# Last chunk of both output projections of a fp32 transformer block: a plain product by token block, each block with its own norm

## The chip, the cores and the metric

The kernel runs on one core of a Trainium2 chip. The metric is the device time of one execution in microseconds. In names of engines: PE is TensorE, DVE is VectorE, ACT is ScalarE, POOL is GpSimd, SP is SyncE, which issues the DMAs.

## What is computed

A block on 1024 latent tokens and 256 context tokens of width 1024, all in fp32. Both feed-forward networks (FFN1 and FFN2) are half-step SwiGLU networks with a hidden width of 2816; between them stands a mixer. FFN2 and the final norm are wanted for the latent tokens only.

```python
def rmsnorm(x, g):
    xf = x.astype(jnp.float32)
    n = xf * lax.rsqrt(jnp.mean(xf * xf, axis=-1, keepdims=True) + EPS)
    return (n * g.astype(jnp.float32)).astype(x.dtype)
...
def swiglu(y, w_in, w_out):
    gate, up = jnp.split(y @ w_in, 2, axis=-1)
    return (jax.nn.silu(gate) * up) @ w_out
```

Per layer: x += gate * swiglu(y) with y the modulated RMSNorm of x (FFN1); then the mixer on a new norm of x; then FFN2 in the same form; then a last RMSNorm to the output. A norm needs the sum of squares over all 1024 features of a token, so it can begin only when the output projection has finished every feature of that token.

## The kernel before

Activations lie transposed: features on partitions, tokens along the free dimension. The latent tokens are two blocks of 512 (tb 0 and 1), the context one of 256 (tb 2). An fp32 product is three products of split operands (high by high, high by low, low by high), each a step of a 128x128 weight piece by 512 columns.

Both projections of an FFN use a scheme of Strassen and Winograd: 7 products of half-size blocks in place of 8. `winograd` (L467) runs the jobs and issues the steps (L479). Its left operands are sums of weight quarters: `unit` (L369) makes them of two loaded pieces, with copies on ScalarE (L389, L393, L396, L403) and sums and differences on GpSimd (L383, L384) for the output projection. Its right operands are sums of the hidden blocks: `combos` (L410) forms them with VectorE and `hl` (L429, L430) splits them; seven tiles of 512 KB per pair are spilled to `hd` (L581).

The output projection runs in chunks of 1, 2, 2, 2, 2, 2 pairs. Each chunk has four jobs, loads its hidden tiles `hc` (L702: 14 of them for two pairs) and, in FFN1, the context's `cc` (L708). Class `Out` says what becomes of the products: VectorE adds each to an accumulator from PSUM (L512, the names a, b, c, f are PSUM banks), the product that several outputs need is summed in `u` and folded into three accumulators in the chunk before the last. In the last chunk it is added three times directly; each output is then finished (L625: x = acc * gate + x), squared on ScalarE and summed over features (`tail`, L461 and L463). Two context products of the last chunk are put off to the end.

After all jobs comes one norm for both blocks: column sums on TensorE (`rstd_cols`, L265, 16 products one column wide), a reciprocal root by 12 small VectorE operations on 8 columns (L279 to L255), its spreading over the partitions on TensorE (L288, 16 products), and then for FFN1 the norm itself (L327 to L334), whose result y the mixer's products `z` take (L356), or for FFN2 the outputs (L1403 to L1414).

The order of instructions on each engine, SyncE's DMA issues included, is decided by a scheduler that simulates a timeline; the pools (32 large tiles d, 7 h, 8 m, 6 PSUM banks for products) limit it. A queue is worked off strictly in its order, so an instruction that waits holds all behind it on that engine.

## Time and profile before

| | us |
|---|---|
| median of 3 runs | 2185.55 (2184.21 to 2193.85) |
| profiled execution | 2185.07 |
| its span in the trace | 2183.3 |
| TensorE busy | 2016.1 (92%) |
| VectorE busy | 1541.3 (71%) |
| ScalarE busy | 832.8 (38%) |
| GpSimd busy | 420.2 (19%) |

The share of busy time is an average over stages with different limits. FFN1's output projection lies from about 645 to 940 us, its last chunk from 868 to 927.5; the mixer follows to about 1475 us and FFN2's first product starts at 1479.0; its output projection lies from about 1919 to 2160, the last chunk from 2110 to 2153.2. The execution's 2185.07 us are the span of 2183.3 and 1.8 us outside the trace.

### The profile page before, as it was taken

How to read it: one execution, taken by the hardware profiler on the slowest of the kernel's cores; microseconds unless marked ns; L12 is line 12 of the kernel's file. 1: busy time of each engine (PE TensorE's matmuls, PEld its weight loads, DVE VectorE, ACT ScalarE, POOL GpSimd, SP SyncE). 2: the span in 40 equal slices, each digit the busy share in tenths (PEclk: the TensorE clock that was granted, in tenths of full speed). 3: DMA queues.
4: the chain of work that ended last, by engine and by line, in shares of the span. 5: the costliest groups of instructions: out<-in, count | busy, mean ns of one | idle time of the engine just before them, and what ended most of it. 6: DMA issues, size and time to landing. Idle time of an engine off the chain costs nothing.

```text
span 2183.3 us, 28555 instructions
## 1 busy us (share of the span) xinstructions
PE 2016.1 (92%) x10820; PEld 1669.9 (76%) x10820; DVE 1541.3 (71%) x2543; ACT 832.8 (38%) x1322; POOL 420.2 (19%) x245
## 2 busy tenths in 40 slices
PE   6799999999999999879999998596999999989995
PEld 2678888888887888757788876474888888867884
DVE  3976665656675779979888376679677786755587
ACT  3633333333342121256556345226344443441222
POOL 0000000000025666422210010200000000065762
PEclk9799999999999999979999899798999999999997
DMA  7033333333369687411111125551444343568852
GB/s 282 24 111 131 116 135 126 121 116 116 116 252 390 251 299 279 156 63 54 40 60 53 35 88 214 205 164 39 164 157 161 118 180 127 194 258 340 307 198 77
DMA packets 115881, 344.86 MB, mean 158 GB/s; under 512 B 12960, under 2 KB 15904, under 8 KB 115744
## 3 DMA queue, kind: packets, MB, share of 16 engines
q1 hardware_dynamic: 115744, 343.04, 42.7%
q8 instruction: 85, 1.39, 0.3%
q14 instruction: 52, 0.43, 0.1%
HBM read 237.60 MB, written 105.38 MB: 157 GB/s over the span
## 4 chain that ended last, share of the span: by engine, by line
PE 67%; DVE 17%; DMA 6%; issue 6%; ACT 3%; POOL 1%; SPq 0%; POOLq 0%; DVEq 0%; ACTq 0%
PE c L479 15%; PE a L479 14%; PE f L479 14%; PE b L479 7%; DVE acc L741 4%; DVE acc L512 2%; DMA ar<-in_wb 2%; PE gc L526 2%; PE gc L525 2%; PE gc L524 2%; DMA hc<-hd 2%; PE row L205 1%; DVE junk L168 1%; DVE hl L430 1%; DVE x L625 1%
## 5 line engine op out<-in xcount | busy, mean ns | idle before, releaser
L384 POOL TENSOR_TENSOR gl<-raw,gh 128x1024 fp32r<-128x1024 f32 x22 | 54.1, 2460 | 1168.8 <-ACT gh L389 1157.2
L168 DVE SCALAR_TENSOR_TENSOR junk<-ar,cr 128x512 bf16<-128x512 f32 x160 | 112.6, 704 | 63.7 <-DMA ar<-in_wb 45.1
L389 ACT ACTIVATE gh<-raw 128x1024 fp32r<-128x1024 f32 x66 | 70.0, 1060 | 197.7 <-PE c L479 70.7
L393 ACT ACTIVATE sh<-s 128x1024 fp32r<-128x1024 f32 x66 | 69.8, 1057 | 167.9 <-PE a L479 94.8
L429 ACT ACTIVATE hl<-g 128x512 fp32r<-128x512 f32 x110 | 67.5, 625 | 159.5 <-DVE g L512 152.0
L479 PE MATMUL f<-hl,uh 128*128 128x512 f32 x528 | 126.8, 389 | 0.0
L479 PE MATMUL c<-hl,sh 128*128 128x512 f32 x352 | 112.5, 397 | 11.8 <-ACT hl L429 9.2
L479 PE MATMUL a<-hl,gh 128*128 128x512 f32 x352 | 114.1, 402 | 8.1 <-ACT hl L429 5.6
L479 PEld LDWEIGHTS f<-hl,uh 128*128 128x128 f32 x528 | 99.1, 188 | 20.6
L479 PE MATMUL b<-hl,gh 128*128 128x512 f32 x352 | 112.0, 395 | 1.0 <-ACT hl L429 1.0
L479 PE MATMUL a<-hl,sh 128*128 128x512 f32 x352 | 110.6, 395 | 1.0 <-ACT g L552 1.0
L479 PE MATMUL f<-hl,th 128*128 128x512 f32 x352 | 110.2, 390 | 1.3 <-ACT hl L429 1.3
L479 PE MATMUL c<-hl,th 128*128 128x512 f32 x352 | 109.0, 391 | 0.1
L741 DVE SCALAR_TENSOR_TENSOR acc<-z,par,acc 128x945 f32<-128x945 f32 (+2 forms) x64 | 95.5, 1512 | 12.3 <-ACT acc L763 11.3
L430 DVE TENSOR_TENSOR hl<-g,hl 128x512 fp32r<-128x512 f32 x110 | 76.7, 712 | 32.5 <-ACT hl L429 32.5
L512 DVE TENSOR_TENSOR u<-c,u 128x512 f32<-128x512 f32 x44 | 30.3, 688 | 96.3 <-ACT u L562 96.3
L142 POOL TENSOR_TENSOR wl<-raw,wh 128x1024 fp32r<-128x1024 f32 x20 | 51.2, 2567 | 241.5 <-ACT wh L141 241.3
L479 PEld LDWEIGHTS c<-hl,sh 128*128 128x128 f32 x352 | 67.1, 191 | 27.5 <-ACT hl L429 9.8
L384 DVE TENSOR_TENSOR sl<-s,sh 128x1024 fp32r<-128x1024 f32 x44 | 53.8, 1224 | 45.7 <-PE gc L525 21.9
L479 PEld LDWEIGHTS a<-hl,gh 128*128 128x128 f32 x352 | 67.0, 194 | 22.3 <-ACT hl L429 6.1
L356 PE MATMUL wo<-ah,wo 128*128 128x512 f32 x128 | 52.1, 408 | 30.0 <-DVE x L1322 28.1
L479 PEld LDWEIGHTS a<-hl,sh 128*128 128x128 f32 x352 | 67.2, 191 | 16.0 <-ACT g L552 1.3
(330 smaller groups left out, 6073.2 us busy)
## 6 DMA issues: line engine op xcount, KB each, us to landing
hd<-hl SPq DMA_DIRECT2D x154, 512.0 KB, 3.6
hc<-hd SPq DMA_DIRECT2D x154, 512.0 KB, 7.7
ar<-in_wb SPq DMA_DIRECT2D x112, 256.0 KB, 3.1
raw<-in_ff1i SPq DMA_DIRECT2D x44, 512.0 KB, 3.9
raw<-in_ff2i SPq DMA_DIRECT2D x44, 512.0 KB, 4.4
raw<-in_ff1o SPq DMA_DIRECT2D x22, 512.0 KB, 5.8
raw<-in_ff2o SPq DMA_DIRECT2D x22, 512.0 KB, 5.1
raw<-in_wa SPq DMA_DIRECT2D x16, 512.0 KB, 10.0
```

The lines of the kernel that those rows point to most:

```text
L142: eng.tensor_tensor(out=lo[:, :n], in0=src[:, :n], in1=hi[:, :n].bitcast(F32), op=ALU.subtract)
L168: i = nc.vector.scalar_tensor_tensor(out=self.junk, in0=w, scalar=1.0, in1=cbc[j], op0=ALU.mult, op1=ALU.mult, accum_out=acc[:, h, dt, j:j ...
L356: m = nc.tensor.matmul(out, a_, xh[k], start=(i == 0), stop=False)
L384: sub = lambda o, x, y: eng.tensor_tensor(out=o, in0=x, in1=y, op=ALU.subtract)
L389: nc.scalar.activation(gh, g, AF.Copy)
L393: nc.scalar.activation(sh, s, AF.Copy)
L429: nc.scalar.activation(t[:, :512], src, AF.Copy)
L430: nc.vector.tensor_tensor(out=t[:, 512:], in0=src, in1=t[:, :512].bitcast(F32), op=ALU.subtract)
L479: mm = lambda x, y, start, stop: nc.tensor.matmul(ps, x, y, start=start, stop=stop, skip_group_check=more)
L512: tt = lambda eng, o, x, y, op: eng.tensor_tensor(out=o, in0=x, in1=y, op=op)
L524: nc.tensor.matmul(ps, hi[:, c], mh, start=i == 0, stop=False)
L741: self.nc.vector.scalar_tensor_tensor(out=o, in0=zv[:, r0 + dr:r1 + dr, c0 + dc:c1 + dc], scalar=self.par[:, tap:tap + 1], in1=o, op0=ALU. ...
```

## The change

The last chunk of both output projections no longer uses the seven products. `last` computes it as a plain product of eight blocks: for each token block it loads four hidden tiles, and for each of eight feature tiles it sums 12 steps of 512 columns in one PSUM bank. `more` adds the result, times the gate, directly from PSUM to x. `halves` replaces `unit` there: the weight pieces are only split, not summed (2 copies, 2 subtracts per unit). As soon as a token block has its eight tiles, `done(tb)` runs its norm alone; the context follows as a third block in FFN1. The folding of `u` and the finishing of the accumulators move from the last chunk to the one before it and to the loop over block 0. The hidden tiles of the last two pairs are spilled as four plain blocks (no `combos`). Accumulators and x tiles are kept by pairs of features and token block.

```diff
+    def halves(self, src, eng, new):
+        nc = self.nc
+        r = {}
+        for x, (i, j) in zip(src, ((1, 2), (0, 4))):
+            x = self.load(x)
+            hi, lo = new("vh", F32R), new("vl", F32R)
+            with self.tc.high_priority():
+                nc.scalar.activation(hi, x, AF.Copy)
+                eng.tensor_tensor(out=lo, in0=x, in1=hi.bitcast(F32), op=ALU.subtract)
+            r[i], r[j] = (hi[:, :512], lo[:, :512]), (hi[:, 512:], lo[:, 512:])
+        return r
...
+        pairs0 = NF // 2 - CHUNKS[-1]
...
+                    if pair >= pairs0:
+                        out(5, b12)
+                        out(7, b22)
+                        return
...
             def p2(s, b):
-                i = add(s.acc(s.m, 0), b, False)
+                i = add(xsum(s.m, 0), b, False)
                 if after_out:
                     after_out(s.j, i)
-                if s.last:
-                    s.finish(s.m, 0)
+                if s.fold:
+                    finish(s.m, 0)
                 if yc:
-                    if s.put_off:
-                        later.append(s.ctx)
-                    else:
-                        s.ctx()
+                    s.ctx()
...
-                if s.last:
-                    for dt, tb in ((m + 4, 1), (m, 1), (m + 4, 0)):
-                        add(s.acc(dt, tb), a, False)
-                else:
-                    add(us[m], a, s.one)
-                add(s.acc(m + 4, 1), c, s.one)
-                add(s.acc(m + 4, 1), f, False)
-                if s.last:
-                    s.finish(m + 4, 1)
+                add(us[m], a, s.one)
+                add(xsum(m + 4, 1), c, s.one)
+                add(xsum(m + 4, 1), f, False)
...
-                add(s.acc(m, 1), c, s.one)
-                add(s.acc(m + 4, 0), f, s.one)
-                if s.chunk == len(CHUNKS) - 2:
-                    for dt, tb in ((m, 1), (m + 4, 0), (m + 4, 1)):
-                        o = s.acc(dt, tb)
-                        tt(nc.vector, o, o, us[m], ALU.add)
-                if s.last:
-                    s.finish(m, 1)
-                    s.finish(m + 4, 0)
-                    tail(m)
-                    tail(m + 4)
+                add(xsum(m, 1), c, s.one)
+                add(xsum(m + 4, 0), f, s.one)
+                if s.fold:
+                    fold_u(m + 4, 0)
+                    finish(m + 4, 0)
...
+        def fold_u(dt, tb):
+            o = xsum(dt, tb)
+            tt(nc.vector, o, o, us[dt % 4], ALU.add)
+        def more(x, ps, dt, j):
+            nc.vector.scalar_tensor_tensor(out=x, in0=ps, scalar=gates()[:, dt, j:j + 1], in1=x,
+                                           op0=ALU.mult, op1=ALU.add)
+        def finish(dt, tb):
+            if (dt // 2, tb) not in xt:
+                xt[dt // 2, tb] = load_x(dt // 2, tb)
+            self.x[dt][tb] = xt[dt // 2, tb][:, dt % 2 * 512:dt % 2 * 512 + 512]
+            more(self.x[dt][tb], xsum(dt, tb), dt, 0)
...
+        def last():
+            kd = CHUNKS[-1]
+            ws = [self.halves(w2[NFO - kd + q], nc.gpsimd, (self.w, self.m)[q % 2 == 0]) for q in range(kd)]
+            tiles = [(q * (4 // kd) + m, i, ws[q], m * kd * P) for q in range(kd) for m in range(4 // kd)
+                     for i in range(2)]
+            rows = lambda w, i, col: [(*w[r], slice(col + k * P, col + k * P + P)) for r in ((1, 2), (0, 4))[i]
+                                      for k in range(kd)]
+            for tb in range(2):
+                right = []
+                for i in ((1, 2), (5, 7))[tb]:
+                    for pair in range(pairs0, NF // 2):
+                        t = self.d("hc", F32R)
+                        nc.sync.dma_start(t.bitcast(F32), hd[pair, names.index(i)])
+                        right.append((t[:, :512], t[:, 512:]))
+                for m, i, w, col in tiles:
+                    dt = m + 4 * i
+                    ps = self.po("o") if i else self.pg("o")
+                    plain(ps, rows(w, i, col), right)
+                    more(self.x[dt][tb], ps, dt, 0)
+                    tail(dt, tb)
+                    if tb == 0:
+                        fold_u(dt, 1)
+                        finish(dt, 1)
+                    elif yc:
+                        finish_c(dt)
+                done(tb)
+            if yc:
+                cs = []
+                for pair in range(pairs0, NF // 2):
+                    t = self.m("cc", F32R)
+                    nc.sync.dma_start(t.bitcast(F32), hc[pair])
+                    cs.append(t)
+                right = [(t[:, h:h + 256], t[:, h + 256:h + 512]) for h in (0, 512) for t in cs]
+                for m, i, w, col in tiles:
+                    dt = m + 4 * i
+                    if i == 0:
+                        pc = self.po("oc")
+                    ps = pc[:, i * 256:i * 256 + 256]
+                    plain(ps, rows(w, i, col), right)
+                    more(self.x[dt][2], ps, dt, 1)
+                done(2)
         p0, n, nj = 0, 0, 0
-        for ci, kd in enumerate(CHUNKS):
+        for ci, kd in enumerate(CHUNKS[:-1]):
...
         self.winograd(jobs)
-        for ctx in later:
-            ctx()
+        last()
...
+        def done1(tb):
+            if "c2" not in late:
+                late["c2"] = self.norm_coef(3, C_N2, 2, "2")
+            self.alloc_y(y2, tb)
+            r = self.rstd(part(2)) if tb == 2 else self.rstd_cols([accs[tb]], 512, 1.0 / 1024.0)
+            self.norm(part(tb), late["c2"], y2, r, pool=True)
...
+        def done2b(tb):
+            bc = self.spread(self.rstd_cols([accs[tb]], 512, 1.0 / 1024.0), 4)
+            b0 = self.h("bc")
+            nc.scalar.activation(b0, bc, AF.Copy)
+            for k in range(NK):
+                g = self.par[:, C_FG + k:C_FG + k + 1]
+                o = self.h("out")
+                if tb and k % 3 == 2:
+                    nc.scalar.activation(o, self.x[k][tb], AF.Identity, scale=g)
+                    nc.gpsimd.tensor_tensor(out=o, in0=o, in1=b0, op=ALU.mult)
+                else:
+                    nc.vector.scalar_tensor_tensor(out=o, in0=self.x[k][tb], scalar=g, in1=bc,
+                                                   op0=ALU.mult, op1=ALU.mult)
+                nc.sync.dma_start(a["out"][k, :, tb * 512:tb * 512 + 512], o)
```

The scheduler places all of this anew. On TensorE at the end of FFN1, before, `st` (column sums), `bc` (spreading) of both blocks stand behind the last context product `oc`, and the mixer's `z` behind them:

```order
L524 MATMUL oc_1157_7588<-cc_1089_7116,uh_1132_7363 128x256
L525 MATMUL oc_1157_7588<-cc_1089_7116,uh_1132_7363 128x256
L526 MATMUL oc_1157_7588<-cc_1089_7116,uh_1132_7363 128x256
L265 MATMUL st_1158_7620<-ones_72,acc_1113_7310 128x1 x4
L265 MATMUL st_1158_7620<-ones_72,acc_1114_7312 128x1 x4
L288 MATMUL bc_1168_7650<-ident_70,r_1159_7629 128x128 x4
L288 MATMUL bc_1185_7699<-ident_70,r_1159_7629 128x128 x4
L356 MATMUL z_1247_7892<-y_1160_7642,wh_1224_7854 128x512
L356 MATMUL z_1248_7919<-y_1160_7642,wh_1229_7862 128x512
```

On TensorE at the same place after, `o` are PSUM banks of the plain product; the first five rows end block 0, `hc_1121` is the first hidden tile of block 1:

```order
L539 MATMUL o_1100_7247<-hc_1081_7105,vh_1076_7095 128x512
L540 MATMUL o_1100_7247<-hc_1081_7105,vh_1076_7095 128x512
L541 MATMUL o_1100_7247<-hc_1081_7105,vl_1077_7096 128x512
L266 MATMUL st_1110_7276<-ones_72,acc_1083_7121 128x1 x4
L289 MATMUL bc_1112_7294<-ident_70,r_1111_7281 128x128 x4
L539 MATMUL o_1125_7343<-hc_1121_7335,vh_1067_7077 128x512
L540 MATMUL o_1125_7343<-hc_1121_7335,vh_1067_7077 128x512
L541 MATMUL o_1125_7343<-hc_1121_7335,vl_1068_7078 128x512
L539 MATMUL o_1129_7364<-hc_1121_7335,vh_1070_7083 128x512
```

The norm of block 0 has moved ahead of all products of block 1.

On SyncE at the end of FFN1, before, the loads of the last hidden tiles and of the last unit's weight halves (`raw` from `in_ff1o`) stood among loads of x and one spill of x to `xd`:

```order
L702 DMA hc_1086_7110<-hd_116_504 128x1024
L702 DMA hc_1087_7112<-hd_116_504 128x1024
L131 DMA raw_1122_7351<-in_ff1o 128x1024
L1355 DMA x_1102_7160<-in_xT 128x512 x2
L126 DMA c_1104_7192<-in_cT 128x1024
L126 DMA c_1105_7193<-in_cT 128x1024
L1355 DMA x_1108_7241<-in_xT 128x512 x2
L1260 DMA xd_7619<-x_1102_7160 128x512
L1355 DMA x_1111_7261<-in_xT 128x512 x2
L1355 DMA x_1119_7345<-in_xT 128x512 x2
L131 DMA raw_1123_7353<-in_ff1o 128x1024
L1355 DMA x_1134_7393<-in_xT 128x512 x2
```

After, the loads of block 1's hidden tiles stand behind eight spills of x tiles of block 0, of which six are shown:

```order
L1311 DMA xd_7751<-x_1032_6707 128x512
L1311 DMA xd_7751<-x_1039_6835 128x512
L1310 DMA xd_7751<-x_1056_6905 128x512
L1310 DMA xd_7751<-x_1063_7033 128x512
L1311 DMA xd_7751<-x_1056_6905 128x512
L1311 DMA xd_7751<-x_1063_7033 128x512
L714 DMA hc_1121_7335<-hd_116_504 128x1024
L714 DMA hc_1122_7337<-hd_116_504 128x1024
L714 DMA hc_1123_7339<-hd_116_504 128x1024
L714 DMA hc_1124_7341<-hd_116_504 128x1024
```

The spills wait for block 0's results, the last one for its last update, and the loads have moved behind them; the weight halves are all issued further ahead.

On TensorE at the end of FFN2, before, the norm of both blocks stands behind the last product:

```order
L479 MATMUL c_2705_17299<-hc_2649_16984,th_2687_17164 128x512 x2
L479 MATMUL c_2705_17299<-hc_2649_16984,tl_2688_17165 128x512
L479 MATMUL f_2706_17300<-hc_2650_16986,uh_2689_17166 128x512 x3
L479 MATMUL f_2706_17300<-hc_2651_16988,uh_2689_17166 128x512 x3
L265 MATMUL st_2712_17355<-ones_72,acc_2670_17114 128x1 x4
L265 MATMUL st_2712_17355<-ones_72,acc_2671_17116 128x1 x4
L288 MATMUL bc_2714_17377<-ident_70,r_2713_17364 128x128 x4
L288 MATMUL bc_2715_17382<-ident_70,r_2713_17364 128x128 x4
```

After, block 0's column sums stand inside the third tile of block 1:

```order
L540 MATMUL o_2660_17162<-hc_2653_17123,vh_2605_16883 128x512
L541 MATMUL o_2660_17162<-hc_2653_17123,vl_2606_16884 128x512
L266 MATMUL st_2640_17072<-ones_72,acc_2621_16927 128x1 x4
L539 MATMUL o_2660_17162<-hc_2654_17125,vh_2605_16883 128x512
L540 MATMUL o_2660_17162<-hc_2654_17125,vh_2605_16883 128x512
```

Its spreading stands 38 rows further on, inside the sixth tile, and only block 1's own norm is left at the end:

```order
L539 MATMUL o_2670_17247<-hc_2655_17127,vh_2614_16901 128x512
L540 MATMUL o_2670_17247<-hc_2655_17127,vh_2614_16901 128x512
L541 MATMUL o_2670_17247<-hc_2655_17127,vl_2615_16902 128x512
L266 MATMUL st_2672_17264<-ones_72,acc_2657_17143 128x1 x4
L289 MATMUL bc_2674_17282<-ident_70,r_2673_17269 128x128 x4
```

Half of the norm has moved from behind the last product to between products.

## Rows read from the trace of the kernel before

**Rows 1.** By stretch: us, busy us per engine, TensorE's clock, DMA share:
```profile
core 0: us, PE busy (x) PEld busy (x) DVE busy (x) ACT busy (x) POOL busy (x), PEclk, DMA share, GB/s
820.00:868.00 48.00, 48.00 (x259) 41.59 (x258) 44.22 (x92) 8.04 (x9) 29.51 (x18) 1.00 0.74 268
868.00:927.50 59.50, 53.27 (x267) 44.40 (x265) 57.34 (x77) 13.04 (x18) 26.51 (x15) 0.94 0.50 175
927.50:960.00 32.50, 16.01 (x58) 13.62 (x58) 27.66 (x52) 17.47 (x28) 9.12 (x6) 0.63 0.29 98
1000.00:1180.00 180.00, 166.10 (x1426) 147.28 (x1425) 160.15 (x204) 96.29 (x182) 30.24 (x12) 0.98 0.16 51
2071.00:2110.00 39.00, 39.00 (x173) 32.02 (x172) 29.63 (x39) 7.42 (x8) 29.32 (x17) 1.00 0.66 251
2110.00:2153.20 43.20, 38.86 (x164) 29.78 (x162) 43.13 (x60) 9.39 (x14) 17.30 (x8) 1.00 0.14 54
2153.20:2183.30 30.10, 7.30 (x32) 6.97 (x32) 16.40 (x34) 8.12 (x13) 7.51 (x6) 0.61 0.36 139
```

**Rows 2.** Chain of waits, steady stretch: start, us, what:
```profile
129.03 2.72 PE c L479 x12
```

**Rows 3.** TensorE's waits, 820 to 962 us: total, times, longest:
```profile
PE st L265 <- DVE acc L463: 11.1, 1, 11.1
PE f L479 <- ACT th L396: 5.8, 1, 5.8
...
PE bc L288 <- DVE r L255: 2.5, 1, 2.5
```

**Rows 4.** Timeline of TensorE, end of FFN1: start, us, instruction, idle before:
```profile
899.71 1.22 PE L479 MATMUL f<-hc,th 128*128 128x512 f32 x2 [5.77 <-ACT th L396]
...
903.70 0.39 PE L479 MATMUL c<-hc,tl 128*128 128x512 f32 x1
...
938.61 3.58 PE L265 MATMUL st<-ones,acc 128*128 128x1 f32 x16 [11.10 <-DVE acc L463]
944.66 3.65 PE L288 MATMUL bc<-ident,r 128*128 128x128 f32 x16 [2.48 <-DVE r L255]
...
958.33 0.39 PE L356 MATMUL ogu<-y,wh 128*128 128x512 f32 x1
```

**Rows 5.** VectorE on acc, 2105 to 2165 us: ns min/median/max, first and last start:
```profile
L512 DVE TENSOR_TENSOR acc<-a,acc x16: 675/680/690, 2109.4 to 2147.4; 128x512 f32<-128x512 f32 x16
L625 DVE SCALAR_TENSOR_TENSOR x<-acc,hg,x x16: 735/744/1691, 2112.2 to 2156.7; 128x512 f32<-128x512 f32 x16
...
L512 DVE TENSOR_TENSOR acc<-acc,u x5: 693/1073/2889, 2105.4 to 2117.3; 128x512 f32<-128x512 f32 x5
```

**Rows 6.** DMA issues of the page: KB each, median us to landing:
```profile
hc<-hd SPq DMA_DIRECT2D x154, 512.0 KB, 7.7
```

**Rows 7.** TensorE's waits, 2040 to 2160 us:
```profile
PE c L479 <- DVE acc L512: 2.6, 3, 2.0
PE f L479 <- DVE acc L512: 1.3, 1, 1.3
```

**Rows 8.** Timeline of VectorE, the last outputs:
```profile
2177.28 2.24 DVE L1412 SCALAR_TENSOR_TENSOR out<-x,par,bc 128x512 f32<-128x512 f32 x3 [0.55 <-DMA out_x<-out]
```

**Rows 9.** TensorE's waits, 630 to 680 us (FFN1, start of the output projection):
```profile
PE oc L524 <- DVE u L512: 2.2, 1, 2.2
PE a L479 <- DMA hc<-hd: 1.9, 1, 1.9
PE f L479 <- DVE acc L512: 0.9, 1, 0.9
```

**Rows 10.** TensorE's waits, 1915 to 1965 us (FFN2, start of the output projection):
```profile
PE c L479 <- ACT acc L607: 3.9, 1, 3.9
PE f L479 <- DVE u L512: 1.1, 1, 1.1
```

**Rows 11.** Timeline of ScalarE, end of FFN2:
```profile
2156.81 0.63 ACT L461 ACTIVATE sq<-x 128x512 f32<-128x512 f32 x1 [0.74 <-DVE acc L463]
```

More of the change, by code (lines that the diff above doesn't have):

```diff
@@ L456, in squares, with tail @@
         nc = self.nc
-        def tail(dt):
-            for tb in range(2):
-                sq = self.sv("sq") if tb in accs else self.tile(self.sb, 512, "ar", "acc")
-                nc.scalar.activation(sq, self.x[dt][tb], AF.Square)
-                if tb in accs:
-                    nc.vector.tensor_tensor(out=accs[tb], in0=accs[tb], in1=sq, op=ALU.add)
-                else:
-                    accs[tb] = sq
+        def tail(dt, tb):
+            sq = self.sv("sq") if tb in accs else self.tile(self.sb, 512, "ar", "acc")
+            nc.scalar.activation(sq, self.x[dt][tb], AF.Square)
+            if tb in accs:
+                nc.vector.tensor_tensor(out=accs[tb], in0=accs[tb], in1=sq, op=ALU.add)
+            else:
+                accs[tb] = sq
         return tail
@@ L505, in winograd, with ffn @@
             job[3].end(c, f)
-    def ffn(self, mov, yc, w1, w2, gates, load_x, load_c, tail, after_out=None):
+    def ffn(self, mov, yc, w1, w2, gates, load_x, load_c, tail, done, after_out=None):
         nc = self.nc
@@ L610, in ffn, with __init__ @@
         class Out:
[L611 to L626 removed]
+            def __init__(s, j, m, w, col, kd, right, chunk):
+                s.j, s.m, s.w, s.col, s.kd, s.right = j, m, w, col, kd, right
+                s.one, s.fold = chunk == 0, chunk == len(CHUNKS) - 2
             def ctx(s):
@@ new lines, in finish_c @@
+        def finish_c(dt):
+            if "c" not in xt:
+                xt["c"] = load_c()
+            self.x[dt][2] = xt["c"][dt // 4][:, dt % 4 * 256:dt % 4 * 256 + 256]
+            more(self.x[dt][2], csum(dt), dt, 1)
+        def last():
[39 more added lines that the diff above has]
+                done(2)
@@ L716, in ffn @@
                 for m in range(4 // kd):
-                    end = ci == len(CHUNKS) - 1 and q == kd - 1
-                    o = Out(nj, q * (4 // kd) + m, w, m * kd * P, kd, right, ci, end)
+                    o = Out(nj, q * (4 // kd) + m, w, m * kd * P, kd, right, ci)
                     jobs.append((w, m * kd * P, right, o))
```

83 lines of the change are left out of this document (21 added, 62 removed).

## Prediction

> **What bounds the kernel now.** I read the busy time by stretch first, then TensorE's waits in the same stretches, then single rows. In both output projections TensorE is full in the chunk before the last: 48.00 of 48 us in FFN1 and 39.00 of 39 in FFN2 [rows 1]. There a 512-column product step costs 2.72 us for 12, so 0.2267 us each [rows 2]. In the last chunk the picture turns. VectorE is full (57.34 of 59.5 us and 43.13 of 43.2), TensorE is not (53.27 and 38.86) [rows 1]. Behind it stands a stretch in which TensorE does hardly anything: 16.01 busy of 32.5 us at a granted clock of 0.63 in FFN1, 7.30 of 30.1 at 0.61 in FFN2 [rows 1]. So the ends of both projections are bound by a chain: VectorE works off its adds, then column sums, the reciprocal root, the spreading of it, and the elementwise work. In FFN1 TensorE waits 11.1 us for the last add of squares and 2.5 for the root, and before that 5.8 us for the weight split of the last unit [rows 3]. That is what a change here can win; in the steady part it can only lose, since each added product lies on the path.
>
> **Products.** Before, the last chunk is 4 jobs of 7 products of 6 steps, 168 steps of 512 columns. The plain form is 2 blocks of 8 tiles of 12, 192 steps. So 24 steps more, x 0.2267 = **+5.4 us in each FFN**, wholly on TensorE. The context products are the same 96 half-width steps.
>
> **FFN1's end.** What goes:
> - The 5.8 us wait for the split of the last unit [rows 3], and what follows it: TensorE did 9 steps from 899.71 to 903.70 [rows 4], 0.44 us each and so at the lower of its two clock levels, 1.2 GHz; 4.0 us for the work of 2.0. The new split is 2 copies and 2 subtracts per unit instead of a chain of sums. Its loads stand behind VectorE results of the chunk before, over 20 us ahead of use. I take all 7.8 us as gained.
> - The end: the last product ends at 927.5, and until 958.33, where steps are fast again [rows 4], 30.8 us pass in which 17 steps of z are done, worth 17 x 0.2267 = 3.9. Lost: 26.9 us.
>
> What comes. In the new order the norm of block 0 (four column sums, four spreads) stands on TensorE ahead of every product of block 1, so TensorE waits out that chain once, with all of block 1's products queued behind it and VectorE's updates behind those. It is: the last update of x 0.74 and the add 0.68 [rows 5], its square 0.63 [rows 11], four column sums (a quarter of 3.58, 0.9 [rows 4]), the root 2.5 [rows 3], four spreads (a quarter of 3.65, 0.9 [rows 4]): 6.4 us. Beside it run the four loads of block 1's hidden tiles. In SyncE's order they stand behind spills of x that need the last update of block 0: 0.74 and then a landing of 7.7 [rows 6], 8.4 us in all. I take 7.4, between the two. After the 5.8 us wait the clock was low and cost 2.0 us; I charge the same again. The sums and spreads of block 1 now stand between other products, 1.8 us. VectorE: the chunk before (44.22 us busy [rows 1]) takes over 16 finishes at 0.74, and block 0 adds 8 updates at 0.74 and 7 adds of squares at 0.68, so 44.2 + 11.8 + 5.9 + 4.8 = 66.7 us against TensorE's 48 + 8 x 2.72 = 69.8. That is tight; I charge 2 us for a backlog (0 to 8). Sum of FFN1: 5.4 - 7.8 - 26.9 + 7.4 + 2.0 + 1.8 + 2 = **-16.1 us**.
>
> The Trainium skill ("DMA: Bandwidth & Descriptors", section "Rules for kernel authors") advises to issue a transfer early and to wait for it late. Block 1's loads do the opposite. By that rule the gap is 8.4 and not 6.4, and the total below would be a microsecond higher than with the value I took; no row of before shows this gap.
>
> This lead is carried to the mixer. From 1000 to 1180 TensorE is busy 166.10 of 180 us and VectorE 160.15 [rows 1], both with hardly a reserve, and the order of the mixer's instructions is nearly unchanged, so a shift of its start should move its end. I carry it whole.
>
> **FFN2's end.** Products +5.4. The waits for PSUM banks in the last chunk, 2.6 + 1.3 [rows 7], come from VectorE being full; it now has 16 updates and 14 adds of squares besides what is left of folds, at most 33 us in 43.5. I leave 1.5 of them: -2.4. The tail was 30.1 us [rows 1]. Now block 0's norm runs beside block 1's products (sums in its third tile, spreads in its sixth, seven outputs before its last updates). After the last product are left: update, square, add 2.1; sums 0.9; root 2.5; spreads 0.9; six outputs on VectorE at 0.75 [rows 8] 4.5; and from the last output to the end 2183.3 - 2179.5 = 3.8 [rows 8]. That is 14.7, and 1.5 for queueing behind block 0's outputs: 16.2, so -13.9. The finishes moved into the chunk before: 29.63 + 11.8 = 41.4 us of VectorE against 39 of TensorE [rows 1], which six PSUM banks can partly hide: +2 (0 to 8). Sum of FFN2: 5.4 - 2.4 - 13.9 + 2 = **-8.9 us**.
>
> **From hidden to output projection.** The last two pairs no longer form their combined operands: 5 VectorE adds, 3 splits and 3 spills of 512 KB less per pair. At this passage TensorE waits 2.2 + 1.9 + 0.9 us in FFN1 [rows 9] and 3.9 + 1.1 in FFN2 [rows 10], in part behind VectorE adds and copies that follow those operands. I take 3 of the 10 us, with bounds 0 and 8.
>
> **Sum.** -16.1 - 8.9 - 3.0 = -28.0 against the profiled run of 2185.07 us: **2157 us**. That run is half a microsecond under the median of 2185.55, so I read the forecast against either. Own range of this case: with every favourable bound (gap 6.4 with no low clock and no backlog, FFN2 without the 2 and the 1.5, passage 8) about 2144; with the unfavourable ones (gap 8.4, backlogs of 8 in both, passage 0) about 2173.
>
> **Rival 1, the lead is swallowed.** The mixer waits for something that doesn't move with its start: its weight loads and splits, or VectorE, 89% busy from 1000 to 1180 [rows 1]. Then FFN1's 16 us shrink to little, and 2185.1 - 8.9 - 3.0 = 2173 is left. For it: VectorE's share. Against it: TensorE is at 92% there, and DMA has a share of only 0.16.
>
> **Rival 2, slower: VectorE held by GpSimd in the chunk before the last.** Adds that read PSUM took 675 to 690 ns throughout FFN2's last chunk; adds of two SBUF tensors (folds of u) had a median of 1073 and up to 2889, finishes up to 1691 [rows 5], while GpSimd's subtracts ran. The change puts 12 folds and 16 finishes, all with two SBUF inputs, into the chunk before the last and block 0, where GpSimd still has some 12 operations per FFN: eight of the last Winograd unit, four of the new splits. If each of the 24 holds one VectorE operation by 2889 - 693 = 2.2 us, that is 53 us; the reserve is 69.8 - 66.7 = 3.1 in FFN1 and, counted the same way, 39 + 21.8 - 52.1 = 8.7 in FFN2. So +41 on the forecast: 2198. It turns slower than before when (28 + 11.8) / 2.2 = 18 of the 24 do so. Against it: half of the 16 finishes took 744 ns or less though GpSimd was busy 17.30 of those 43 us [rows 1], and the new updates read PSUM. The Trainium skill ("GPSIMD Engine Reference", section "8. Key points") says that GpSimd shares its SBUF interfaces with VectorE, with contention for instructions that have two SBUF inputs. By that rule every meeting of the two costs, and the 2198 would be nearer; the rows agree on which instructions suffer, not that all do.
>
> **Rival 3, more is won.** The passage gives all of its 8 us and the backlogs don't appear: 2157 - 5 - 4 = 2148.
>
> **How the numbers follow.** Chances: forecast 0.58, rival 1 0.18, rival 3 0.12, rival 2 0.09, and 0.03 for something unseen at about no change. About 0.5% (10.9 us, so 2174.6 and 2196.5) is what a measurement of this kernel can tell from no change. Faster takes the forecast, rival 3 and most of rival 1 (0.13): 0.83. Same takes the rest of rival 1, the 0.03 and the lower part of rival 2 (0.04): 0.12. Slower 0.05. The range goes from 2144 to 2177: it leaves out the worst of rival 1, rival 2 and a little below, some 0.2 in all.
>
> **What would show it.** In FFN1: one idle stretch of TensorE of 6 to 9 us between two runs of plain products, released by the root or by a hidden-tile load, then steps of 0.44 for some microseconds, and no wait for a weight split. The first z some 16 us earlier, and the same lead at FFN2's start. In FFN2: column sums of block 0 without a wait, and 16 us from the last product to the end. If the idle stretch is over 12 us, or folds and finishes of 2 us and more line up before it, the FFN1 term is wrong; if the lead at the mixer's end is not that at its start, the carrying is.

## The result and the profile after

The changed kernel takes **2156.62 us** (median of 4 runs, 2152.53 to 2159.04) against 2187.28 of the kernel before beside it (4 runs, 2184.21 to 2193.85): a ratio of 0.9854 with a 95% interval of 0.9825 to 0.9883. The forecast was 2157 within 2144 to 2177. So time and sign came out as predicted, in part by luck: the terms for the two FFNs' ends were 7.7 us too favourable together, and 9.2 us that the forecast didn't count came from elsewhere in the profiled execution.

In the changed kernel `ffn` records with other line numbers: the Winograd steps are L492 (L479 before), the steps of the plain product L539 to L541, VectorE's adds L526, updates and finishes of x L686, adds of squares L476, `st` L266, `bc` L289. Busy time by stretch of the changed kernel, to be set against [rows 1] (PE busy, PEld, DVE, ACT, POOL, then TensorE's clock):

```profile
core 0: us, PE busy (x) PEld busy (x) DVE busy (x) ACT busy (x) POOL busy (x), PEclk, DMA share, GB/s
2039.87:2083.69 43.82, 39.68 (x161) 31.84 (x160) 37.75 (x46) 6.66 (x7) 26.75 (x13) 0.92 0.65 232
2083.69:2128.30 44.61, 44.61 (x206) 37.21 (x205) 30.34 (x52) 9.46 (x15) 2.41 (x1) 1.00 0.00 0
2128.30:2153.80 25.50, 10.28 (x45) 8.49 (x43) 15.40 (x32) 4.13 (x7) 2.49 (x2) 0.69 0.43 165
...
892.30:899.80 7.50, 2.78 (x17) 2.67 (x17) 3.40 (x14) 0.63 (x1) 0.00 (x0) 0.73 0.75 244
899.80:930.00 30.20, 30.20 (x155) 25.82 (x154) 25.10 (x40) 12.85 (x20) 5.64 (x4) 0.95 0.31 124
930.00:960.00 30.00, 30.00 (x164) 25.56 (x163) 21.45 (x43) 18.26 (x31) 11.31 (x6) 1.00 0.23 71
```

In FFN1 the hole at the end, 16.01 busy of 32.5 us before [rows 1], is gone: from 899.8 to 960 TensorE is unbroken, through block 1, context, norms and into the mixer. What is left is one hole of 7.5 us between the two blocks. In FFN2 TensorE is full in the plain product (44.61 of 44.61) and VectorE no longer is (30.34, where it was 43.13 of 43.2); the hole of the last chunk has moved forward into the chunk before it (39.68 of 43.82).

The timeline of TensorE in the changed kernel shows the hole between the blocks, and the one at the end of FFN2 (start, us, instruction, idle time before it and its releaser):

```profile
894.61 1.05 PE L266 MATMUL st<-ones,acc 128*128 128x1 f32 x8 [2.29 <-DVE acc L476]
898.10 2.07 PE L289 MATMUL bc<-ident,r 128*128 128x128 f32 x8 [2.43 <-DVE r L256]
...
2134.31 0.39 PE L541 MATMUL o<-hc,vl 128*128 128x512 f32 x1
2138.42 1.83 PE L266 MATMUL st<-ones,acc 128*128 128x1 f32 x8 [3.73 <-DVE acc L476]
2142.78 2.05 PE L289 MATMUL bc<-ident,r 128*128 128x128 f32 x8 [2.52 <-DVE r L256]
```

### The profile page after: what moved, and what is told of

It reads as the page before. It is cut to its first block, busy times and chain, and to the rows that moved or that the text cites. A ratio compares the mean times of both kernels' runs of the same rounds, so it can differ in the third digit from the quotient of the medians.

```text
span 2153.8 us, 28445 instructions
## 1 busy us (share of the span) xinstructions
PE 2015.6 (94%) x10868; PEld 1669.6 (78%) x10868; DVE 1503.2 (70%) x2503; ACT 816.5 (38%) x1297; POOL 379.9 (18%) x215
## 4 chain that ended last, share of the span: by engine, by line
PE 72%; DVE 18%; DMA 5%; issue 2%; ACT 2%; POOL 0%; SPq 0%; DVEq 0%; ACTq 0%
PE c L492 14%; PE a L492 14%; PE f L492 14%; PE b L492 7%; DVE acc L791 3%; DMA ar<-in_wb 2%; PE gc L541 2%; PE gc L540 2%; PE gc L539 2%; PE row L206 1%; DVE hl L444 1%; PE o L541 1%; PE o L539 1%; PE o L540 1%; DVE junk L169 1%
## 5 line engine op out<-in xcount | busy, mean ns | idle before, releaser
L384 POOL TENSOR_TENSOR s<-raw 128x512 f32<-128x512 f32 x18 | 23.8, 1322 | 1149.0 <-DVE ch L526 602.0
L492 PE MATMUL f<-hl,uh 128*128 128x512 f32 x528 | 126.8, 389 | 0.0
L492 PE MATMUL a<-hl,gh 128*128 128x512 f32 x352 | 114.4, 403 | 8.8 <-ACT hl L443 6.3
L492 PE MATMUL c<-hl,sh 128*128 128x512 f32 x352 | 111.1, 393 | 11.7 <-ACT hl L443 9.6
L492 PEld LDWEIGHTS f<-hl,uh 128*128 128x128 f32 x528 | 99.1, 188 | 20.6
L492 PE MATMUL b<-hl,gh 128*128 128x512 f32 x352 | 112.3, 396 | 0.8 <-ACT hl L443 0.8
L492 PE MATMUL a<-hl,sh 128*128 128x512 f32 x352 | 110.1, 393 | 1.0 <-ACT g L567 1.0
L492 PE MATMUL f<-hl,th 128*128 128x512 f32 x352 | 110.2, 390 | 0.8 <-ACT hl L443 0.8
L492 PE MATMUL c<-hl,th 128*128 128x512 f32 x352 | 108.9, 391 | 0.0
L526 DVE TENSOR_TENSOR u<-c,u 128x512 f32<-128x512 f32 x44 | 30.2, 687 | 109.0 <-ACT u L577 109.0
L791 DVE SCALAR_TENSOR_TENSOR acc<-z,par,acc 128x945 f32<-128x945 f32 (+2 forms) x64 | 93.1, 1477 | 11.6 <-ACT acc L813 10.5
L492 PEld LDWEIGHTS c<-hl,sh 128*128 128x128 f32 x352 | 66.4, 189 | 27.4 <-ACT hl L443 10.2
L492 PEld LDWEIGHTS a<-hl,gh 128*128 128x128 f32 x352 | 67.1, 195 | 23.0 <-ACT hl L443 6.8
L492 PEld LDWEIGHTS b<-hl,gh 128*128 128x128 f32 x352 | 67.3, 191 | 15.8 <-ACT hl L443 1.8
L492 PEld LDWEIGHTS a<-hl,sh 128*128 128x128 f32 x352 | 66.6, 189 | 15.7 <-ACT g L567 1.3
```

Of the source, the lines that this page charges most:

```text
L492: mm = lambda x, y, start, stop: nc.tensor.matmul(ps, x, y, start=start, stop=stop, skip_group_check=more)
L791: self.nc.vector.scalar_tensor_tensor(out=o, in0=zv[:, r0 + dr:r1 + dr, c0 + dc:c1 + dc], scalar=self.par[:, tap:tap + 1], in1=o, op0=ALU. ...
```

## Where the time went: five sections of the trace

For every kernel that follows I cut the span at the last start of four groups of products: the hidden projection of FFN1 (`f<-hl,uh`), `z` and `wo` of the mixer, the hidden projection of FFN2. So "FFN1 end" holds FFN1's whole output projection, the norm and the `z` products, and "mixer" lies from the last `z` to the last `wo`. A section's length is the difference of two cuts. The two cuts of the mixer are read from these rows of the changed kernel (count, ns min/median/max, first and last start; the last starts are 1094.2 and 1449.0):

```profile
L360 PE MATMUL z<-y,wl x176: 277/389/632, 926.3 to 1094.2; 128*128 128x512 f32 x128, 128*128 128x256 f32 x48
...
L360 PE MATMUL wo<-ah,wo x128: 388/389/628, 1325.1 to 1449.0; 128*128 128x512 f32 x128
```

| kernel | median us | ratio to before, 95% | start | FFN1 end | mixer | FFN2 hidden | FFN2 end |
|---|---|---|---|---|---|---|---|
| before | 2187.28 | 1 | 639.6 | 470.7 | 364.7 | 450.5 | 257.8 |
| after | 2156.62 | 0.9854 [0.9825, 0.9883] | 634.1 | 460.1 | 354.8 | 456.7 | 248.1 |
| f1_only | 2167.40 | 0.9915 [0.9889, 0.9942] | 634.1 | 460.0 | 359.0 | 453.1 | 259.2 |
| f2_only | 2178.04 | 0.9954 [0.9936, 0.9973] | 639.9 | 470.7 | 365.0 | 453.0 | 248.1 |
| joint | 2155.79 | 0.9860 [0.9831, 0.9889] | 634.9 | 457.4 | 347.3 | 457.1 | 253.0 |
| early | 2135.01 | 0.9761 [0.9731, 0.9791] | 638.3 | 450.0 | 346.4 | 458.2 | 242.9 |
| early_f1 | 2141.24 | 0.9793 [0.9766, 0.9820] | 634.9 | 450.9 | 343.3 | 458.6 | 248.2 |
| split_dve | 2149.35 | 0.9831 [0.9795, 0.9868] | 633.6 | 453.4 | 354.5 | 456.3 | 242.2 |
| early_split | 2130.14 | 0.9744 [0.9712, 0.9777] | 633.4 | 449.6 | 345.9 | 458.9 | 241.0 |
| combos_kept | 2158.22 | 0.9872 [0.9841, 0.9903] | 633.5 | 464.1 | 342.5 | 455.5 | 255.5 |
| extra | 2163.92 | 0.9897 [0.9870, 0.9924] | 637.2 | 472.4 | 335.3 | 461.4 | 257.8 |
| before_mods | 2181.32 | 0.9983 [0.9964, 1.0002] | 636.0 | 470.8 | 364.1 | 451.3 | 260.7 |
| early_mods | 2134.95 | 0.9768 [0.9740, 0.9796] | 633.5 | 452.4 | 350.7 | 454.5 | 243.6 |

Each ratio is to before as measured beside that kernel (medians from 2186.42 to 2188.16). The section lengths are from one profiled execution of each kernel. Many repeat to 0.1 us where the code is the same: FFN1's end 470.7, 470.7 and 470.8 in before, f2_only and before_mods, 460.0 and 460.1 in f1_only and after, FFN2's end 248.1, 248.1 and 248.2 in f2_only, after and early_f1. Not all do: the old FFN2 end took 257.8, 259.2 and 260.7 us in before, f1_only and before_mods, and FFN1's end 450.0 and 450.9 in early and early_f1. So these lengths tell more than a median, which scatters by several microseconds, but a difference of less than 3 us in one section shows nothing.

After less before: start -5.5, FFN1 end -10.6, mixer -9.9, FFN2 hidden +6.2, FFN2 end -9.7; sum -29.5, the difference of the spans. The 5.5 us arise before 131 us, where nothing is changed. After is 1.8 us ahead already at early column sums (55.88 us in before, 54.07 in after) and 3.1 at 113 us. Another 2.8 come behind that, of which 0.4 are lost again later: in before and f2_only TensorE's granted clock was 0.62 and 0.64 from 117 to 124 us, behind two waits of 1.4 and 1.0 us that after has too, while it was 1.00 there in after. After, early and extra, with the same code in this section, started FFN1's end at 634.1, 638.3 and 637.2, so most of the 5.5 us may be chance of single executions. Whether the medians hold any of it no run tells.

## The experiments

**Each FFN by itself.** f1_only keeps the old FFN2, f2_only the old FFN1 (functions `ffn_w` and `squares_w` are those of before):

```diff
+        self.ffn_w(mov, None, a["ff2i"], a["ff2o"], gates2, load_x2, None, self.squares_w(accs),
+                 self.ada_todo((8,), 1, 1, 16))
...
-        self.ffn(mov, None, a["ff2i"], a["ff2o"], gates2, load_x2, None, self.squares(accs),
-                 done2b, self.ada_todo((8,), 1, 1, 16))
```

> The change in FFN1's last chunk alone; FFN2 as before. Theory A (the accounting of the trace of after: FFN1's part is worth 17 us, namely 14.0 at its end, 4.9 more in the mixer, 1.9 lost at the passage; 5.8 us of the two profiles' difference arose in code that is the same in both): about 2170 against 2187 of before. Theory B (the prediction's own terms, 16.1 in FFN1 and nothing in the mixer): also about 2170, but the mixer's wait for the gate modulation, 23.3 us before and 11.6 after, stays at about 23.

> The change in FFN2's last chunk alone; FFN1 as before. Theory A: 6.7 us gained (4.2 at the passage, 11.0 at the end, 8.5 lost in the chunk before the last): about 2180.5, and the mixer's wait of 23 us as before. Theory B (prediction: 8.9 and half of the passage's 3): about 2177. A rival on the chunk before the last: if TensorE's wait of 4.1 us there belongs to the shifted phase of FFN1 and not to FFN2's own change, it is gone here and the gain is 11 to 15 us.

Measured beside 2188.16 of before: 2167.40 and 2178.04, so -20.8 and -10.1, together -30.9, and the whole change had -30.7. The two halves add up, within the scatter. By sections, f1_only wins 10.7 at FFN1's end and 5.7 in the mixer, which its diff doesn't touch; f2_only wins 9.7 at FFN2's end. The longest wait of `wo` in the mixer is 11.1 us in f1_only (11.6 in after) and 23.5 in f2_only (23.3 before), so the mixer's new length comes with the change in FFN1. In f2_only's chunk before the last TensorE still waits 2.6 and 1.9 us for adds, so this wait belongs to FFN2's own change, and f2_only's rival falls.

**The price of a step.** extra repeats one block of each sum: 15 steps per tile in place of 12, 48 steps more in each FFN. It thereby computes another sum than the reference; it only prices the steps.

```diff
-                    plain(ps, rows(w, i, col), right)
+                    plain(ps, rows(w, i, col) + rows(w, i, col)[:1], right + right[:1])
```

> After, with the first block of each plain product's sum multiplied once more: 15 steps per tile in place of 12, 2 blocks x 8 tiles x 3 = 48 steps more in each FFN (the context's products have the extra block too, 8 x 3 half-width steps in FFN1). The output is not the reference's; the run only prices steps. Theory A (each step of the plain product lies on TensorE's path, as the prediction priced the 24 steps of the change): 2 x 48 x 0.2267 = 21.8 us and 8 x 3 x half of it = 2.7 us, so 2156.6 + 24.5 = 2181, and 2 to 8 us less where a longer tile lets VectorE's backlog in the fold chunk and block 0 go: 2173 to 2181. Rival (VectorE sets the pace of the last chunk, so that a step there costs little): 2158 to 2166.

Measured: 2163.92, 7.3 over after. By its time alone that is the rival's result. The sections say otherwise. FFN1's end grew by 12.3 us and FFN2's by 9.7, where 48 x 0.2267 = 10.9 are worked out for each if the steps lie on the path. (The expectation adds 2.7 us for the context in FFN1, which is wrong: the edit leaves the context's products alone, 96 half-width steps in both kernels.) So a step costs what the prediction took. What hid it is the mixer: it was 19.5 us *shorter* than in after, though no product of it is changed, while FFN2's hidden projection was 4.7 longer. TensorE's wait in the mixer that differs most is the one of `wo` for VectorE's update of x (total, times, longest), of extra:

```profile
PE wo L357 <- DVE x L1372: 6.7, 6, 2.0
```

of after:

```profile
PE wo L357 <- DVE x L1372: 19.5, 13, 11.6
```

and of before:

```profile
PE wo L356 <- DVE x L1322: 28.1, 10, 23.3
```

So the mixer is not always merely shifted. Over all runs its length goes from 335.3 to 365.0 us, and the length goes with the order that the scheduler gave it. TensorE's order of products in the mixer, by the names in the traces, is the same in after, f1_only and split_dve, and their mixers took 354.8, 359.0 and 354.5 us; before and f2_only share one (364.7 and 365.0), and early, early_f1 and early_split another, but for two neighbouring products (346.4, 343.3 and 345.9). Extra, combos_kept and joint each have an order of their own. Where the order is the same, a lead, that is an earlier start, passes through: split_dve is 7.2 us ahead of after at the last `z` and 7.5 at the last `wo`. Between before and after TensorE's order differs in a few neighbouring products only, but VectorE's dot products and updates of x stand in another order, and the wait above is 8.6 us shorter. No run changes the order alone, so that it is the cause is likely and not shown.

**Moving the work that `wo` waits for.** The update of x needs the mixer's gate, whose dot products of weights (VectorE, 0.68 us each) before and after run late. before_mods and early_mods (before, and the kernel early described below) issue them ahead of the second group of the mixer's queries:

```diff
-        g1 = self.gla(1)
-        q1 = [self.queries(1, dt) for dt in range(2)]
...
-        for ch in (5, 6, 7):
+        for h in range(2):
+            for dt in range(NK):
+                self.ada_part(5, dt, h, [row[:, h * 512:h * 512 + 512]])
+        g1 = self.gla(1)
+        q1 = [self.queries(1, dt) for dt in range(2)]
+        for ch in (6, 7):
```

> Before, with one thing moved: the VectorE dot products of the mixer's gate modulation (16 of them, 0.70 us each) stand earlier in the mixer, so that the modulation is ready long before the mixer's output products need it. Theory A (TensorE's wait of 23.3 us in the mixer's output projection is an accident of where the scheduler put these dot products, and the change to be explained shortened it to 11.6 by the same accident): the single long wait is gone, 2175 to 2182 against 2188. Rival (what is late next, the attention outputs or VectorE's additions, takes its place): under 3 us, 2185 to 2188.

> The kernel with early loads of block 1's hidden tiles, and the gate modulation moved earlier as well. There the modulation was ready in time already (no wait over 1.9 us in the mixer's output projection, 12.1 in twelve pieces). Theory A: little is left to win there, 2131 to 2136 against 2135. Rival (the pieces come from the dot products between VectorE's additions): 5 to 10 us less, 2125 to 2130.

The wait of `wo` fell from 28.1 to 1.2 us and from 12.1 to 1.5. The time hardly did: 2181.32 against 2186.42, which is inside theory A's range but with an interval that holds 1, and 2134.95 against early's 2135.01. The mixer kept its length in before_mods (364.1 against 364.7): the last `ogu` products came at 1338.2 in place of 1322.4. Where the saved wait went is seen in TensorE's busy time and clock over the mixer, of before (first row) and of before_mods, and in one stretch of before_mods (the third):

```profile
core 0: us, PE busy (x) PEld busy (x) DVE busy (x) ACT busy (x) POOL busy (x), PEclk, DMA share, GB/s
1110.30:1475.00 364.70, 324.78 (x2738) 269.64 (x2737) 247.53 (x495) 150.59 (x249) 43.00 (x24) 0.92 0.36 121
...
1106.80:1470.90 364.10, 340.68 (x2737) 287.16 (x2736) 254.99 (x495) 152.01 (x250) 43.58 (x24) 0.88 0.37 121
...
1246.80:1276.80 30.00, 30.00 (x199) 25.25 (x201) 14.88 (x46) 6.63 (x11) 0.00 (x0) 0.50 0.43 134
```

TensorE idled 16.5 us less (23.4 in place of 39.9) and was busy 15.9 us more with the same products: for 30 us, behind 10 us with 7.40 busy, it was granted only the lower of its two levels. early_mods shows the same beside early (330.88 us busy in place of 320.92, clock 0.90 in place of 0.95). So the long wait marks the mixers that take long, but it isn't by itself the cause: taken away here, it came back as slower steps. What sets the mixer's length in each order stays open.

**The norm of each block.** joint keeps the plain product but issues both norms behind all products in the program:

```diff
-                done(tb)
+            if not yc:
+                done(0)
+                done(1)
...
+                done(0)
+                done(1)
```

> The plain product kept, but the norms of both token blocks only after all latent products (in FFN1 after the context's too). Theory A (most of the gain is VectorE's relief: no backlog of adds behind the last product, so the chain is short even when it is joint): FFN2's tail grows by about 7 us (outputs of both blocks after the last product), FFN1 loses its idle stretch of 7.6 us between the blocks and pays about as much at the end: 2160 to 2166. Rival (the gain is the overlap of block 0's norm alone; the plain product by itself only costs its 10.9 us): 2180 to 2195.

Measured: 2155.79, the same as after and less than either theory expected. In FFN2 the edit does what it says: the sums of both blocks stand behind the last product, and FFN2's end is 4.9 us longer, so the norm beside products is worth about that. Against before, joint wins 4.8 us there. So about half of FFN2's gain comes without any overlap of the norms: from the rest of the change, that is the plain product, whose results go straight to x, the weights that are only split, and the operands that are no longer formed (the last experiment prices these alone). In FFN1 the scheduler undid the edit in part: it put block 0's sums between the context's products (start, us; then the group of these products, first and last start):

```profile
914.23 0.50 PE L266 MATMUL st<-ones,acc 128*128 128x1 f32 x4
918.99 0.50 PE L266 MATMUL st<-ones,acc 128*128 128x1 f32 x4
...
L541 PE MATMUL oc<-cc,vl x32: 279/283/283, 911.6 to 923.6; 128*128 128x256 f32 x32
```

TensorE no longer stops between the blocks, and FFN1's end is not longer but 2.7 us shorter, a difference within the scatter; against before it wins 13.3. So a stop between the blocks is not needed for FFN1's gain; what that gain would be without any overlap joint does not show. The mixer, in another order, was 7.5 us shorter.

**The gap between the blocks.** early issues block 1's hidden loads right behind block 0's, early_f1 in FFN1 alone:

```diff
+            rights = []
             for tb in range(2):
                 right = []
...
+                rights.append(right)
+            for tb in range(2):
+                right = rights[tb]
```

> After, with the hidden tiles of block 1 issued right behind those of block 0 in the program; in its order the column sums of block 0 then stand in the third tile of block 1 in FFN1 too. Theory A (the idle stretch between the blocks, 7.6 us with norm inside it, and the six slow steps behind it, 1.3 us, lie on the path to the end): 6 to 9 us less than after, 2148 to 2151. Rival (the mixer, VectorE at 89%, swallows a lead): within 2 us of after, 2155 to 2159.

> After, with block 1's hidden tiles loaded right behind block 0's in FFN1 alone; FFN2 as in after. It parts the 21.6 us that the early loads won in both. Theory A (the gain is FFN1's gap, 10 us, and the mixer's order behind it, 7 to 8 us; FFN2 gives 4 to 5): 2138 to 2141. Rival (most of it came from another order of the whole program behind FFN1, so that it does not stand without the edit in FFN2): 2143 to 2152.

early measured 2135.01, 21.6 under after where 6 to 9 were expected, and early_f1 2141.24, 15.4 under after. Both shorten FFN1's end by 10.1 and 9.2. SyncE in after issued block 1's four tiles only behind the last spills (start, us):

```profile
890.87 2.59 SPq L1311 DMA_DIRECT2D xd<-x  x2
893.58 2.05 SPq L714 DMA_DIRECT2D hc<-hd  x4
```

In early one was issued at 831.60 and three at 849.01. With the tiles there, the scheduler puts block 0's norm between block 1's products, and TensorE of early waits for neither sums nor root:

```profile
897.75 0.95 PE L266 MATMUL st<-ones,acc 128*128 128x1 f32 x8
907.09 1.05 PE L289 MATMUL bc<-ident,r 128*128 128x128 f32 x8
```

Its busy time by stretch is full there:

```profile
870.00:930.00 60.00, 59.13 (x307) 50.65 (x308) 48.89 (x91) 18.57 (x29) 8.87 (x5) 1.00 0.33 115
```

The gap of 7.5 us and 1.2 us of slow steps behind it are 8.7 of the 10.1. The Trainium skill ("DMA: Bandwidth & Descriptors", section "Rules for kernel authors") has the rule for it, issue early and wait late; these runs agree. The rule bears on the order here, for in after no product waited for these loads: TensorE stood for the sums and the root, which the scheduler had put in front. The loads took 5.3 to 7.5 us to land, the first was there at 898.9, and block 1 could not have begun before it. Another 8.4 and 11.5 us came in the mixer, in its other order. FFN2's end gained 5.2 in early and nothing in early_f1 (248.2), as it must.

**VectorE and GpSimd.** split_dve does the four subtracts of the weight halves of each FFN on VectorE; early_split is both edits together.

```diff
-            ws = [self.halves(w2[NFO - kd + q], nc.gpsimd, (self.w, self.m)[q % 2 == 0]) for q in range(kd)]
+            ws = [self.halves(w2[NFO - kd + q], nc.vector, (self.w, self.m)[q % 2 == 0]) for q in range(kd)]
```

> After, with the four subtracts per FFN that split the last chunk's weights on VectorE (1.22 us each by the same operation elsewhere) in place of GpSimd. Theory A (a GpSimd subtract holds VectorE's folds and finishes, 2.2 us each, in the chunk before the last): VectorE pays 4.9 us per FFN and is freed of up to 8.8, TensorE's waits of 4.1 and 1.8 us in FFN2 shrink: 2149 to 2155 against 2156.6. Rival (only the number of VectorE operations counts there): the backlog grows by up to 4.9 us per FFN, 2158 to 2166.

> After, with both edits that won: block 1's hidden tiles loaded right behind block 0's, and the 4 subtracts of the weight halves of each FFN on VectorE in place of GpSimd. Theory A (the first removed the gap between the blocks, the second the meetings of VectorE and GpSimd in the fold chunk, which early still has; they add): 2135.0 - 7.3 = 2128, range 2125 to 2131. Rival (early's order already avoids the meetings, or the mixer swallows the second lead as it did with the moved modulation): 2133 to 2137.

In after, the chunk before the last of FFN2 has the collision that rival 2 described. Timeline of VectorE and of GpSimd there:

```profile
2061.33 2.88 DVE L526 TENSOR_TENSOR acc<-acc,u 128x512 f32<-128x512 f32 x1
2064.14 0.68 DVE L526 TENSOR_TENSOR acc<-f,acc 128x512 f32<-128x512 f32 x1
2064.74 2.28 DVE L686 SCALAR_TENSOR_TENSOR x<-acc,hg,x 128x512 f32<-128x512 f32 x1
2066.94 2.82 DVE L526 TENSOR_TENSOR acc<-acc,u 128x512 f32<-128x512 f32 x1
```

```profile
2058.38 5.29 POOL L420 TENSOR_TENSOR vl<-raw,vh 128x1024 fp32r<-128x1024 f32 x2 [4.39 <-ACT vh L419]
2063.98 2.49 POOL L385 TENSOR_TENSOR sl<-s,sh 128x1024 fp32r<-128x1024 f32 x1 [0.31 <-PE c L492]
2066.43 2.79 POOL L385 TENSOR_TENSOR tl<-s,th 128x1024 fp32r<-128x1024 f32 x1
```

Folds and a finish of two SBUF inputs take 2.3 to 2.9 us beside GpSimd, the add from PSUM between them 0.68. TensorE pays with a wait of 4.09 us. The 14 steps behind it, up to 2076.86, take 6.45 us, where at the higher clock level they are worth 3.2:

```profile
2070.41 1.22 PE L492 MATMUL a<-hc,sh 128*128 128x512 f32 x2 [4.09 <-DVE acc L526]
```

In split_dve only this is left of that wait (total, times, longest):

```profile
PE a L492 <- DVE acc L526: 0.8, 1, 0.8
```

FFN1's end is 6.7 and FFN2's 5.9 shorter, with the mixer in the same order. So the place of four subtracts costs 6 to 7 us in each FFN's trace. The median, 2149.35, is 7.3 under after, less than their sum and with ranges that overlap (2141.81 to 2155.72, and 2152.53 to 2159.04); the profiled execution, at 2141.81, was the fastest of four, and what the others lost is not recorded. The rule of the Trainium skill that the prediction cited ("GPSIMD Engine Reference", section "8. Key points") is right on which instructions suffer; the price is what these rows add. early_split measured 2130.14, the lowest median here, 57.8 under before. But of the 4.9 us by which it lies under early, its sections show only 0.4 at FFN1's end and 1.9 at FFN2's, and the ranges of the two overlap, so a gain over early is not shown. Early has the meetings too (14 folds and finishes over 1 us, 15 in after), but its products wait for VectorE's adds at most 1.3 us at a time: a slow VectorE operation costs only where TensorE waits for it.

**The hidden projection's last pairs.** combos_kept forms, splits and spills the old operands of the last two pairs again, unused:

```diff
                     if pair >= pairs0:
                         out(5, b12)
                         out(7, b22)
+                        layer.combos(b11, b12, b21, b22, lambda i, b: None if i in (5, 7) else out(i, b))
                         return
```

> After, with the combined operands of the last two pairs still formed, split and spilled on the engines (nobody reads them), so that the passage from hidden to output projection carries the old work. The prediction put 3 us on this term with bounds 0 and 8; the two profiles showed about 4 us gained at FFN2's passage and none at FFN1's. Theory A: 3 to 5 us slower than after, 2159 to 2162. Rival (the saved work was hidden anyway): 2155 to 2158. Rival (it is worth its 8): 2164 and more.

Measured: 2158.22, 1.6 over after and between the two ranges. By the median the removal is worth next to nothing. The sections show 4.0 at FFN1's end, little more than the scatter, and 7.4 at FFN2's, 11.4 together, and a mixer shorter by 12.3, in another order, that hides them.

## Why the prediction was right, and where not

- **Products, +5.4 per FFN:** the price is borne out by extra, 12.3 and 9.7 us where 10.9 were worked out for each.
- **FFN1's gap, 7.4 us:** right in size, in part by luck. From the last product of block 0 at 891.93 + 0.39 to the first of block 1 at 899.82 are 7.5 us. The value was taken between a norm chain of 6.4 and loads of 8.4; the chain alone took the 7.5: 2.3 to the last add, 1.1 for the sums, 2.4 for the root, 1.7 for the spreads. A block has half of the 16 sums and spreads of [rows 4], not a quarter, so 0.9 for each holds at the higher clock level only. The loads were not waited for; the first landed at 898.9, the last only behind 902. The slow steps behind the gap were 6 of 0.43 us, 1.2 us lost and not 2.0.
- **FFN1's waits that go:** right. No wait for a weight split is left, where 5.8 us stood [rows 3], and the hole at the end is gone.
- **FFN1's backlog, 2 us:** mis-sized. Before block 0's norm TensorE waits four times for VectorE's adds, and some steps are slow behind them:

```profile
856.19 0.73 PE L492 MATMUL c<-hc,th 128*128 128x512 f32 x2 [1.00 <-DVE acc L526]
859.46 0.73 PE L492 MATMUL a<-hc,sh 128*128 128x512 f32 x2 [0.25 <-DVE acc L526]
865.41 0.50 PE L539 MATMUL o<-hc,vh 128*128 128x512 f32 x1 [0.45 <-DVE acc L526]
868.20 1.07 PE L492 MATMUL c<-hc,th 128*128 128x512 f32 x2 [1.36 <-DVE acc L526]
```

  That is 3.1 us and about 1.5 at the lower clock, 4.6 in all.
- **FFN1's term, -16.1:** too large. From the steps ahead of the chunk before the last (820.09 before, 816.23 after) to the last z (1110.3 and 1094.2) 12.2 us were won. The backlog makes 2.6 of the 3.9 that are missing; the rest is not traced.
- **FFN2's term, -8.9:** failed; 2.5 us were won. The step that failed is the +2 for the finishes that moved into the chunk before the last. From the last steps ahead of that chunk (2066.83 before, 2039.87 after) to the same steps in it (2104.92, 2085.51; 2111.04, 2092.53) 8.5 us of lead over before were lost: the collision with GpSimd. That lies just outside the stated bound of 0 to 8; 7.4 of it are the wait of 4.09 and the slow steps behind it. The rest gave -11.0, and 5.4 - 2.4 - 13.9 = -10.9 had been worked out, by two errors that cancelled. From last product to end are 19.1 us and not 16.2: the sums took 1.83 us, and from the start of the spreads to the first output 2.7 passed, where 0.9 stood for each. From 2111.04 and 2092.53 to the last product both kernels took 42.2 us, where 5.4 - 2.4 = 3.0 more had been expected: TensorE's waits there, 4.1 us before, are all gone, and the waits for PSUM banks of [rows 7] don't occur in the plain product.
- **Passage, -3:** mis-sized. From its last hidden product to the steps ahead of the chunk before the last, FFN2 won 7.2 us of lead (from 19.8 to 27.0), while FFN1 lost 1.6 (from 5.5 to 3.9), which is within the scatter. combos_kept gives 11.4 for both together, though in FFN1 not at the passage itself: TensorE's waits from 620 to 700 us are 4.6 in it and 6.2 in after, and more before block 0's norm (sums 4.6 against 2.3).
- **"I carry it whole":** right for the same order, and split_dve shows it (7.2 us ahead of after at the last z, 7.5 at the last wo). The change didn't keep the order, on VectorE above all. The lead over before was 16.1 us at the last z, 26.0 at the last wo and 19.8 at FFN2's last hidden product: the mixer won 9.9 of its own, and FFN2's hidden projection gave 6.2 back. 3.2 of these were lost by the end of the long wait for `hl`, which both kernels have, first before (last `wo` at 1474.97), then after (at 1448.97):

```profile
1501.00 0.80 PE L479 MATMUL c<-hl,sh 128*128 128x512 f32 x1 [9.21 <-ACT hl L429]
...
1478.20 0.79 PE L492 MATMUL c<-hl,sh 128*128 128x512 f32 x1 [9.14 <-ACT hl L443]
```

  Rival 1 was right that the mixer's length is not fixed; that it swallows this lead was wrong, it added 3.7 to it.
- **Rival 2:** its mechanism is there, at another price. Of the 56 folds and finishes of after 15 took over 1 us and nine over 2; before had 21 and nine, so the change moved the meetings and did not add any. Where they make TensorE wait they cost, 6 to 7 us per FFN by split_dve. The reason given against the rival, that half of the finishes were quick beside a busy GpSimd, held: from 2060 to 2140 us their median was 744 ns, that of the folds 692.

Summed up, FFN1 gave 12.2, FFN2 2.5 and the passages 5.6, together 20.3 us (10.6 at FFN1's end and 9.7 at FFN2's), where terms and passage made 28.0. The mixer and FFN2's hidden projection gave 3.7 that had not been counted, and the start 5.5, so that the profiled gain is 29.5. That the forecast hit is luck to this extent. The medians show 30.7, within the scatter of these executions.

## What to carry to other kernels

When a step starts a second block behind a reduction, issue its loads with those of the first: the gap cost 10 us here and was one loop's order. Compare sections of the trace between fixed points and not only totals: extra and combos_kept read by their medians would have given the wrong verdict on a step's price and on the operands, because an untouched section was scheduled anew and gave the time back. But know first how far a section repeats: here to 0.1 us in many cases, to 3 in others. A lead may be carried through a later stage if that stage's instruction order stays the same on every engine. And a wait that is taken away is not yet time won: look whether TensorE's clock keeps its level.

## What the runs showed of the hardware

A subtract of 128x1024 on GpSimd (2.4 to 2.9 us) beside a VectorE add of two SBUF tensors of 128x512 stretches the latter from 0.69 to as much as 2.88 us, while an add from PSUM in the midst of it took 0.68. TensorE's granted clock was at 0.62 from 117 to 124 us in one execution of code that in another, with the same two waits of 1.4 and 1.0 us, kept 1.00; that alone made 2.8 us. In the mixer of before_mods 16.5 us less idle time of TensorE went with 15.9 us more busy time at a mean granted clock of 0.88 in place of 0.92.
